# Other places for the seven-product and eight-product weight pairs of a decoder trunk, and their splits interleaved

## Chip, cores and metric

The kernel runs on one core of one Trainium2 chip. The metric is the device time of one execution in microseconds (us). The kernel before takes 2254.26 us, the median of three runs (2252.91 to 2255.19).

## What is computed

The reference is a decoder trunk of two layers for 256 tokens of width 2048, in fp32. Each layer has a token mixer (HGRN2 in the first, gated linear attention, "GLA", in the second), which shares its input projection with a cross-attention into 256 memory tokens; an output projection; and a SwiGLU feed-forward network of 5632 hidden columns. Cut to what matters:

```
x = x + concat(mixer(norm(x) @ w_in), memory_attention(xq, mem)) @ w_out
g, u = split(norm(x) @ w_gate_up)        # 5632 columns each
x = x + (silu(g) * u) @ w_down
# GLA: q, k (768 columns each), v, g (1536 each), gk_low (16), xq (512) = norm(x) @ w_in
```

In the GLA layer the last 16 + 512 columns of the input projection are the low-rank decay and the queries of the memory attention ("gx" in the kernel); gk0 and gk1 are its key and query columns for two heads each.

## The kernel before

**Products.** Every number is held as a high and a low part (fp32r), and every product of two tiles is three matmuls: high by high, high by low, low by high. A weight is loaded raw into a buffer `raw` of four blocks of 512 columns (three such buffers), and `split` (L276) makes its parts: ScalarE (ACT) casts the high part, VectorE (DVE) subtracts to get the low one. Parts of two blocks lie in one of six buffers, a single block in one of two. The traces call the parts of pair i parts<i>a, b, c and d. TensorE (PE) multiplies and sums in eight PSUM banks.

**Pairs.** Weight rows go by pairs of two tiles of 128 rows, 2048 rows being eight pairs, and two column blocks (gate and up, say) are computed together. A pair of kind "S" goes by a scheme of Strassen and Winograd with seven products (21 matmuls for 256 tokens). Kinds "O" and "H" (and "-" in the mixer) take eight (24 matmuls). The seven products need sums of weights. `seven` (L451) makes them: it splits a single block (a), splits two (b), subtracts in place on `raw` (one block, then two), splits two blocks (c), and splits the last two (d). An O pair needs only a and b, an H pair one subtraction of one block and a third split c besides.

**Loads.** For an S pair of the feed-forward network `load_pair` has SyncE's queue (SP) load one row of blocks (L443), GpSimd's queue (POOL) add a second row onto it as an accumulating transfer (L444), and SP load the rest (L445, L447). The accumulating transfer waits until the first row has landed, and the subtraction on VectorE until both have. An O or H pair has plain loads (L445, L449). For pair 0 of an S-headed block, and for pair 7 where it is S, that sum lies in a tile T of its own, loaded by GpSimd's queue (`load_apart`, L428 and L429).

**Gate and up.** `project_halves` (L624) does 512 gate and 512 up columns as one block; a layer has eleven blocks b. KINDS (L1197) is a table of the kinds of the eight pairs: one entry each for b = 0, 1, 2, 3, and the last one for all after. From block 1 on, `Engine.kept` holds the instructions of TensorE, VectorE and ScalarE in program order, so the order of the code is the order on the engine. The seven sums of a block are combined by VectorE (`sums`, L1223), then gated, transposed and split into the operand of the down projection (L1266), four 512-column pieces per part, two of which run behind each block. These steps fall due at keys (WHEN, L1203) that `mark` passes as the pairs go by. Two down splits per block run on GpSimd (L300) rather than VectorE; each is held back by `free_port` until a certain add of `sums` has run.

**Mixer.** In the GLA layer `gla` (L1139) computes gx by two calls of `project` (four quads of tiles, 264 columns each time, eight products for a pair), `gla_pair` (L1068) computes gk0 and gk1 by `project_two` (L549), with the plan "------S-", one pair on seven. The order of work outside blocks 1 to 10 is a scheduler's.

Of the kernel before, what the change touches and what calls it, by code (L numbers as in the profile page):

```python
# [17 lines left out]
P = 128  # L18
# [22 lines left out]
def trunk_kernel(ctx: ExitStack, tc: tile.TileContext, x, mem, norm_mix, norm_ffn, norm_mem,  # L41
# [234 lines left out]
    def split(src, name, by=2, turned=False):  # L276

        if isinstance(src, list):
            both = wts.tile([P, 2, 2, 512], F32R, tag="parts", name=f"parts{name}", bufs=6)
            for k in (1, 0):  # L280
                hi = both[:, 0, k:k + 1, :]
                ac.activation(out=hi, in_=src[k], func=AF.Copy, scale=-1.0)
                ve.scalar_tensor_tensor(out=both[:, 1, k:k + 1, :], in0=src[k], scalar=-1.0, in1=hi.bitcast(F32),
                                        op0=ALU.mult, op1=ALU.subtract)
            return [(both[:, 0, k, :], both[:, 1, k, :]) for k in range(2)]
# [165 lines left out]
    def seven(i, raw, fed, between=None):  # L451

        n = raw.shape[2]
        tt = ve.tensor_tensor
        b00, = split(raw[:, 0:1, :], f"{i}a")
        b11, b10 = split(raw[:, 2:4, :], f"{i}b")
        if between:
            between()

        if not fed:  # L460
            tt(out=raw[:, 1, :], in0=raw[:, 1, :], in1=raw[:, 2, :], op=ALU.add)
        apart = fed if fed and fed is not True else None
        tt(out=raw[:, 0, :], in0=apart[:, 0, :] if apart else raw[:, 1, :], in1=raw[:, 0, :], op=ALU.subtract)
        tt(out=raw[:, 2:4, :], in0=raw[:, 2:4, :], in1=raw[:, 0:1, :].broadcast_to([P, 2, n]), op=ALU.subtract)
        t6, t7 = split([raw[:, 0:1, :], apart] if apart else raw[:, 0:2, :], f"{i}c", turned=True)
        t5, t4 = split(raw[:, 2:4, :], f"{i}d")
        return {1: ("x00", b00), 2: ("x01", b10), 3: ("z", b11), 4: ("x11", t4), 5: ("s", t5), 6: ("u", t6), 7: ("d0", t7)}
# [81 lines left out]
    def project_two(pairs, plan, w, c0, c1, n, name, give, view=lambda ps: ps, onto=None, prep=None, behind=None,  # L549
# [43 lines left out]
        for at, (p, kind) in enumerate(zip(order, plan)):  # L593
            i, raw = new_raw()
            if i == 0:
                load_pair(raw, w, p, c0, c1, n, kind, fed)
            if prep:
                prep(at)
            if i > 0:
                load_pair(raw, w, p, c0, c1, n, kind, fed)  # L600
            if kind == "S":
                todo = held(behind, seven, i, raw[:, :, 0:n], fed) if behind else seven(i, raw[:, :, 0:n], fed)
                last = at == plan.rindex("S")
                for b in (1, 6, 7, 5, 2, 4, 3) if last else (3, 2, 1, 6, 7, 5, 4):
                    product(b, pairs[p].get(todo[b][0]), todo[b][1])
                if last and at == len(plan) - 1:
                    early()
                elif len(pending) > MANY:
                    step()
                continue  # L610
# [13 lines left out]
    def project_halves(forms, kinds, w, c0, c1, name, key, keep, apart):  # L624
# [15 lines left out]
        for p, kind in enumerate(kinds):  # L640
            Engine.kept = keep <= p
            i, raw = new_raw()
            if p == 4 and kinds[7] == "S":
                apart[7] = load_apart(w, 7, c1)
            fed = apart.get(p, True)
            load_pair(raw, w, p, c0, c1, 512, kind, fed)
            x = forms[p].get
            last = p == len(PAIRS) - 1
            if kind == "S":
                todo = seven(i, raw, fed, lambda: mark(key + p))  # L650
                for b in (1, 2, 6, 7, 5, 4, 3) if last else (1, 3, 2, 6, 7, 5, 4):
                    product(b, x(todo[b][0]), todo[b][1])
            else:
                b00, b01 = split(raw[:, 0:2, :], f"{i}a")
                mark(key + p)
                b11, b10 = split(raw[:, 2:4, :], f"{i}b")
                todo = [[(2, "x00", b00), (5, "x10", b01), (4, "x10", b00), (3, "d0", b01)]]
                if kind == "O":
                    todo.append([(2, "x01", b10), (5, "x11", b11), (4, "x11", b10), (3, "d1", b11)])
                else:  # L660
                    ve.tensor_tensor(out=raw[:, 3, :], in0=raw[:, 3, :], in1=raw[:, 2, :], op=ALU.subtract)
                    e1, = split(raw[:, 3:4, :], f"{i}c")
                    todo.append([(2, "x01", b10), (3, "x01", b11), (7, "x11", b11), (4, "x11", e1)])
# [403 lines left out]
    def gla_pair(w, pr, dec, decay, hq, r, yq):  # L1067
# [46 lines left out]
        project_two(hq["pairs"], ("------S-", "------S-")[pr], w, kw + pr * 2 * DK, pr * 2 * DK, 2 * DK, f"gk{pr}", give,  # L1114
# [24 lines left out]
    def gla(hq, scale, yq):  # L1139
# [11 lines left out]
        psx = [project(hq, range(NQ), w, 3 * MIX + i * half, half, f"gx{i}",  # L1151
                       prep=lambda q: len(got) == 0 and q == 3 and got.append(scale())) for i in range(2)]
# [3 lines left out]
        for t in range(NT):  # L1156
            ac.activation(out=low[:, t, 0:GR], in_=psx[0][t][:, 0:GR], func=AF.Copy, scale=r[:, t:t + 1])
# [30 lines left out]
        attention(1, [[(0, psx[0][t][:, GR:half]), (half - GR, psx[1][t][:, 0:half])] for t in range(NT)], r, yq)  # L1188
# [8 lines left out]
    KINDS = ("SHHSHOSO", "HHHSSOSO", "SHHSSOSO", "SSHSSOHS", "SSSSSOSS")  # L1197
# [10 lines left out]
    def ffn(l, forms, r, after, tail=None):  # L1208
# [9 lines left out]
        def up_block(b):  # L1218
            ps = project_halves(forms, KINDS[min(b, 4)], w_gate_up[l], 512 * b, DFF + 512 * b, f"f{l}_{b}_",
# [4 lines left out]
            def sums():  # L1224
# [4 lines left out]
                for out, p, q in ((s0, 2, e0), (e1, 6, e0), (s1, 7, e1), (e1, 5, e1), (e0, 5, s1),  # L1229
                                  (s1, 4, s1), (e1, 3, e1)):  # L1230
                    ve.tensor_tensor(out=out, in0=ps[p], in1=q, op=ALU.add)
                    if p in (2, 5) and out is not e0 and b:
# [201 lines left out]
```

## Time and profile before

| what | value |
|---|---|
| median of three runs | 2254.26 us |
| the profiled execution, its own time | 2254.6 us |
| span of its instructions | 2252.8 us |
| busy, PE / DVE / ACT / POOL | 99% / 90% / 64% / 12% |
| granted clock of TensorE | 0.999 |
| matmuls recorded | 10668 |
| HBM read | 472.12 MB |

A row of a timeline gives start, duration, engine, line of the kernel, operation, and tiles as out<-in; in brackets stands how long the engine was idle before, and what it was released by. Durations on PE overlap, since matmuls are pipelined; the spacing of their starts is the cost. Rows of VectorE overlap by about 0.1 us in the same way. PEld is the load of a matmul's weights.

### The profile page before, as it was taken

What the parts mean: (1) busy time and instruction counts of PE and PEld (TensorE: products, weight loads), DVE (VectorE), ACT (ScalarE), POOL (GpSimd) and SP (SyncE); (2) the same over time, 40 slices, a digit from 0 to 9 for tenths busy, and PEclk for the clock granted to TensorE, in tenths of its full rate; (3) what the DMA queues carried; (4) which work ended last, traced back from release to release, by engine and by line L of the source; (5) the groups of instructions that cost most, each with busy time, mean ns of one, the idle gap of its engine ahead of it and who ended that gap; (6) DMA issues with size and microseconds to landing.
All of it is one profiled execution on the core that took longest, in us unless ns stands there. A gap on an engine that the chain in (4) does not pass through costs nothing.

```text
span 2252.8 us, 30400 instructions
## 1 busy us (share of the span) xinstructions
PE 2238.6 (99%) x10668; PEld 1894.6 (84%) x10668; DVE 2031.5 (90%) x2551; ACT 1452.8 (64%) x2010; POOL 280.4 (12%) x275
## 2 busy tenths in 40 slices
PE   9999999999999999999999999999999999999998
PEld 7888888888888888888889999988888888888887
DVE  6879899898998999999996887889999999999997
ACT  7656656565666666666665665566566676666664
POOL 1000100000111112112210000000011221212110
PEclk9999999999999999999999999999999999999999
DMA  8656655656687778878865445566677878887874
GB/s 296 215 168 213 199 182 177 200 193 190 198 236 232 229 234 231 230 230 238 244 221 168 141 156 182 164 209 197 208 221 224 233 230 238 242 238 236 231 233 167
DMA packets 255628, 477.28 MB, mean 212 GB/s; under 512 B 18255, under 2 KB 47731, under 8 KB 255219
## 3 DMA queue, kind: packets, MB, share of 16 engines
q1 hardware_dynamic: 228547, 420.21, 55.5%
q0 software_dynamic: 25632, 50.87, 13.0%
q10 hardware_dynamic: 1296, 4.26, 0.5%
q8 instruction: 84, 1.38, 0.2%
q14 instruction: 69, 0.57, 0.1%
HBM read 472.12 MB, written 3.15 MB: 211 GB/s over the span
## 4 chain that ended last, share of the span: by engine, by line
PE 90%; DVE 6%; issue 2%; DMA 1%; ACT 1%; SPq 0%; POOL 0%; DVEq 0%; POOLq 0%; ACTq 0%
PE f_p L151 34%; PE fd L151 18%; PE wo L151 4%; PE m1p L151 2%; PE hv2p L151 2%; PE hv1p L151 2%; PE hf0p L151 2%; PE hv0p L151 2%; PE wo1p L151 2%; PE hf2p L151 2%; PE hf1p L151 2%; PE wo0p L151 2%; PE m0p L151 2%; PE gk0p L151 1%; PE gk1p L151 1%
## 5 line engine op out<-in xcount | busy, mean ns | idle before, releaser
L151 DVE TENSOR_TENSOR raw<-raw 128x1024 f32<-128x1024 f32 (+3 forms) x330 | 311.2, 943 | 16.7 <-DMA raw<-in_w_down_dram 5.6
L151 ACT CAST parts<-raw 128x1024 fp32r<-128x1024 f32 (+1 forms) x216 | 211.7, 1016 | 56.8 <-DMA raw<-in_w_down_dram 14.7
L151 DVE TENSOR_TENSOR parts<-raw,parts 128x1024 fp32r<-128x1024 f32 (+1 forms) x176 | 200.2, 1171 | 22.7 <-ACT parts L151 22.0
L444 POOL DMA_DIRECT2D raw<-in_w_gate_up_dram x92 | 80.4, 873 | 541.2 <-DMA raw<-in_w_gate_up_dram 274.7
L300 POOL TENSOR_TENSOR parts<-raw,parts 128x1024 fp32r<-128x1024 f32 x40 | 95.6, 2406 | 113.5 <-ACT parts L151 81.2
L151 ACT COPY h<-fd 128x512 f32<-128x512 f32 x80 | 45.7, 588 | 46.5 <-PE fd L151 44.0
L428 POOL DMA_DIRECT2D T<-in_w_gate_up_dram x36 | 21.1, 587 | 430.2 <-DVE hf_4g L151 82.7
L151 ACT ACTIVATE s<-s,rf_r 128x512 f32<-128x512 f32 x44 | 31.8, 723 | 42.0 <-DVE s L151 42.0
L151 DVE SCALAR_TENSOR_TENSOR s<-e,rf_r,s 128x512 f32<-128x512 f32 x44 | 45.7, 1076 | 2.9 <-ACT s L151 0.5
L151 DVE TENSOR_TENSOR e<-f_p,e 128x512 f32<-128x512 f32 x66 | 45.2, 684 | 2.6 <-DVE s L151 0.5
L429 POOL DMA_DIRECT2D T<-in_w_gate_up_dram x36 | 31.0, 861 | 120.4 <-DMA T<-in_w_gate_up_dram 111.1
L151 ACT COPY fd<-h 128x512 f32<-128x512 f32 x82 | 45.2, 582 | 0.0
L444 POOL DMA_DIRECT2D raw<-in_hgrn_w_in_dram x17 | 14.7, 867 | 209.9 <-DMA raw<-in_hgrn_w_in_dram 124.6
L151 PE MATMUL fd<-parts,s_0h 128*128 128x512 f32 x128 | 39.8, 392 | 0.0
L151 PE MATMUL fd<-parts,s_4h 128*128 128x512 f32 x128 | 39.8, 392 | 0.0
L151 PE MATMUL fd<-parts,s_8h 128*128 128x512 f32 x128 | 39.8, 392 | 0.0
L151 PE MATMUL fd<-parts,s_2h 128*128 128x512 f32 x128 | 39.8, 392 | 0.0
L151 PE MATMUL fd<-parts,s_6h 128*128 128x512 f32 x128 | 39.8, 392 | 0.0
L151 PE MATMUL fd<-parts,s_1h 128*128 128x512 f32 x128 | 39.4, 389 | 0.0
L151 PE MATMUL fd<-parts,s_3h 128*128 128x512 f32 x128 | 39.4, 389 | 0.0
L151 PE MATMUL fd<-parts,s_5h 128*128 128x512 f32 x128 | 39.4, 389 | 0.0
L151 PE MATMUL fd<-parts,s_7h 128*128 128x512 f32 x128 | 39.4, 389 | 0.0
(6020 smaller groups left out, 7434.0 us busy)
## 6 DMA issues: line engine op xcount, KB each, us to landing
raw<-in_w_gate_up_dram SPq DMA_DIRECT2D x224, 512.0 KB, 4.4
raw<-in_w_down_dram SPq DMA_DIRECT2D x80, 1024.0 KB, 5.5
raw<-in_w_gate_up_dram SPq DMA_DIRECT2D x220, 256.0 KB, 4.2
raw<-in_hgrn_w_in_dram SPq DMA_DIRECT2D x79, 512.0 KB, 4.6
raw<-in_gla_w_in_dram SPq DMA_DIRECT2D x96, 384.0 KB, 3.3
raw<-in_w_gate_up_dram POOLq DMA_DIRECT2D x92, 256.0 KB, 4.9
T<-in_w_gate_up_dram POOLq DMA_DIRECT2D x72, 256.0 KB, 5.0
raw<-in_w_out_dram SPq DMA_DIRECT2D x16, 1024.0 KB, 5.1
```

The source lines that it names most:

```text
L151: ins = func(*args, **kwargs)
L300: low = (nc.gpsimd if free_port else ve).tensor_tensor(out=both[:, 1, k:j, 0:m], in0=src[:, k:j, :], in1=both[:, 0, k:j, 0:m].bitcast(F32) ...
L428: nc.gpsimd.dma_start(out=both[:, 0, :], in_=rows[0])
L429: nc.gpsimd.dma_start(out=both[:, 0, :], in_=rows[1], accum_op=ALU.add)
L444: nc.gpsimd.dma_start(out=raw[:, 1, 0:n], in_=rows[1], accum_op=ALU.add)
```

## The change

1. *The next S pair's start is interleaved.* `seven` gets a function `ahead`, called between its splits c and d (and in an H pair ahead of split c): it takes a buffer, issues the next pair's loads, and makes its split a. A pair that was begun so does its first subtraction ahead of split b. Where the sum lies apart in T, the subtraction on two blocks is put between the two halves of split c.
2. *Order of pairs.* From block 1 on the pairs go 0, 1, 2, 5, 3, 4, 6, 7; the O pair (5) comes fourth instead of sixth.
3. *KINDS.* Blocks 1 and 2 have one S pair more each, in the place of an H pair. Block 3 takes the plan of the blocks after it, two S more. That is four pairs in each of two layers.
4. *GLA projections.* gk0 and gk1 go by "-----SS-", two pairs on seven. gx becomes one call of `project_two` with the same plan for both of its 264-column halves, and the sums end in two tiles of SBUF (tags gate and v) instead of in PSUM.
5. *Sums.* The seven adds run in another order, and GpSimd's two splits are released by the first and the fourth add (e1 + bank 6, e0 + bank 5) instead of the first (s0 + bank 2) and the fourth (e1 + bank 5).

```diff
-    def seven(i, raw, fed, between=None):
+    def seven(i, raw, fed, between=None, b00=None, ahead=None):
...
+        if not begun:
+            b00, = split(raw[:, 0:1, :], f"{i}a")
...
+        if fed and begun:
+            less()
         b11, b10 = split(raw[:, 2:4, :], f"{i}b")
...
+        if not (fed and begun):
+            less()
+        if apart:
+            t6, t7 = split([raw[:, 0:1, :], apart], f"{i}c", turned=True, between=both_less)
+        else:
+            both_less()
+            t6, t7 = split(raw[:, 0:2, :], f"{i}c", turned=True)
+        if ahead:
+            ahead()
         t5, t4 = split(raw[:, 2:4, :], f"{i}d")
...
-        for p, kind in enumerate(kinds):
-            Engine.kept = keep <= p
-            i, raw = new_raw()
...
+        def ahead(at):
+            if at < len(order) and kinds[order[at]] == "S":
+                i, raw = come(at)
+                came.append((i, raw, split(raw[:, 0:1, :], f"{i}a")))
+
+        for at, p in enumerate(order):
+            kind = kinds[p]
+            Engine.kept = keep <= at
+            i, raw, begun = came.pop() if came else (*come(at), None)
...
-        project_two(hq["pairs"], ("------S-", "------S-")[pr], w, kw + pr * 2 * DK, pr * 2 * DK, 2 * DK, f"gk{pr}", give,
+        project_two(hq["pairs"], "-----SS-", w, kw + pr * 2 * DK, pr * 2 * DK, 2 * DK, f"gk{pr}", give,
...
-        psx = [project(hq, range(NQ), w, 3 * MIX + i * half, half, f"gx{i}",
-                       prep=lambda q: len(got) == 0 and q == 3 and got.append(scale())) for i in range(2)]
+        psx = []
...
+        project_two(hq["pairs"], "-----SS-", w, 3 * MIX, 3 * MIX + half, half, "gx", give,
+                    prep=lambda at: at == 4 and got.append(scale()), fed=False)
...
-    KINDS = ("SHHSHOSO", "HHHSSOSO", "SHHSSOSO", "SSHSSOHS", "SSSSSOSS")
+    KINDS = ("SHHSHOSO", "HHSSSOSO", "SSHSSOSO", "SSSSSOSS", "SSSSSOSS")
+
+    ORDERS = ((0, 1, 2, 3, 4, 5, 6, 7), (0, 1, 2, 5, 3, 4, 6, 7))
...
-                for out, p, q in ((s0, 2, e0), (e1, 6, e0), (s1, 7, e1), (e1, 5, e1), (e0, 5, s1),
+                for out, p, q in ((e1, 6, e0), (s0, 2, e0), (s1, 7, e1), (e0, 5, s1), (e1, 5, e1),
                                   (s1, 4, s1), (e1, 3, e1)):
                     ve.tensor_tensor(out=out, in0=ps[p], in1=q, op=ALU.add)
-                    if p in (2, 5) and out is not e0 and b:
+                    if (p == 6 or out is e0) and b:
                         free_port.append(ve.last)
```

On VectorE, in a steady block (5 of the first layer), before: the fourth and fifth pairs, 139 and 140, are S, and the sixth, 141, is O; SCALAR_TENSOR_TENSOR is the split c, raw<-raw are the subtractions.

```order
L151 TENSOR_TENSOR parts139d<-raw_6691,parts139d 128x1024
L151 TENSOR_TENSOR parts140a<-raw_6731,parts140a 128x512
L151 TENSOR_TENSOR parts140b<-raw_6731,parts140b 128x1024
L151 TENSOR_TENSOR raw_6731<-raw_6731 128x512
L151 TENSOR_TENSOR raw_6731<-raw_6731 128x1024
L151 SCALAR_TENSOR_TENSOR parts140c<-raw_6731,parts140c 128x1024
L151 TENSOR_TENSOR parts140d<-raw_6731,parts140d 128x1024
L151 TENSOR_TENSOR parts141a<-raw_6774,parts141a 128x1024
L151 TENSOR_TENSOR parts141b<-raw_6774,parts141b 128x1024
```

The same engine and block after: 139 is now the O pair, 140 and 141 are S.

```order
L151 TENSOR_TENSOR parts138d<-raw_6639,parts138d 128x1024
L151 TENSOR_TENSOR parts139a<-raw_6703,parts139a 128x1024
L151 TENSOR_TENSOR parts139b<-raw_6703,parts139b 128x1024
L151 TENSOR_TENSOR parts140a<-raw_6736,parts140a 128x512
L151 TENSOR_TENSOR parts140b<-raw_6736,parts140b 128x1024
L151 TENSOR_TENSOR raw_6736<-raw_6736 128x512
L151 TENSOR_TENSOR raw_6736<-raw_6736 128x1024
L151 SCALAR_TENSOR_TENSOR parts140c<-raw_6736,parts140c 128x1024
L151 TENSOR_TENSOR parts141a<-raw_6755,parts141a 128x512
L151 TENSOR_TENSOR parts140d<-raw_6736,parts140d 128x1024
L151 TENSOR_TENSOR raw_6755<-raw_6755 128x512
L151 TENSOR_TENSOR parts141b<-raw_6755,parts141b 128x1024
```

The O pair has moved up by two places, split a of pair 141 stands ahead of split d of pair 140, and the first subtraction of 141, which needs both of its accumulated rows, ahead of its split b.

On TensorE, at the start of gx, before: fd is the last down projection of the first layer, tp_hm are the transposes of the mixer's input.

```order
L151 MATMUL fd_5_3_0_1_9861<-parts_2_9919,s_10l 128x512
L151 MATMUL gx_0_0_9957<-parts_0_9961,hm_0x 128x264 x3
L151 MATMUL gx_0_1_9958<-parts_0_9961,hm_0x 128x264 x3
L151 MATMUL gx_0_0_9957<-parts_0_9961,hm_0x 128x264 x3
L151 MATMUL gx_0_1_9958<-parts_0_9961,hm_0x 128x264 x3
L151 MATMUL tp_hm_6_9980<-ident,h 128x128
```

The same place after:

```order
L151 MATMUL fd_5_3_0_1_9873<-parts_2_9931,s_10l 128x512
L151 MATMUL tp_hm_6_9979<-ident,h 128x128
L151 MATMUL tp_hm_7_9989<-ident,h 128x128
L151 MATMUL gxp_9998<-parts216a,hm_2x 128x264 x3
L151 MATMUL gxp_10002<-parts216a,hm_2x 128x264
```

The twelve matmuls of gx that stood between the last fd and the first transpose have moved behind it.

On VectorE, at the end of gx, after (gxgate and gxv are the two tiles of its sums; before, no such row stood there):

```order
L151 TENSOR_TENSOR parts224a<-raw_10301,parts224a 128x2x384
L151 TENSOR_TENSOR gxgate<-gxp_9998,gxgate 128x264
L151 TENSOR_TENSOR gxgate<-gxp_10002,gxgate 128x264
L151 TENSOR_TENSOR gxv<-gxp_10006,gxv 128x264
L151 TENSOR_TENSOR gxv<-gxp_10010,gxv 128x264
```

Four adds on VectorE now stand between the last product of gx and the scaling of the queries on ScalarE.

## Prediction before the run

> **What bounds the kernel now.** I read the page first (span, busy shares), then the waits of TensorE, the chain of waits in order of time, the windows of the feed-forward blocks, and last the timelines of one block and of the two places in the mixer that the change touches. Page:
>
> ```profile
> span 2252.8 us, 30400 instructions
> PE 2238.6 (99%) x10668; PEld 1894.6 (84%) x10668; DVE 2031.5 (90%) x2551; ACT 1452.8 (64%) x2010; POOL 280.4 (12%) x275
> ```
>
> TensorE (PE) is busy for 99%, VectorE (DVE) for 90%. What TensorE waited for, with total, times and longest in us:
>
> ```profile
> PE tgk L151 <- ACT gsk L151: 1.4, 2, 0.8
> PE tp_hm L151 <- DVE h L151: 1.0, 2, 0.8
> PE f_p L151 <- DVE parts96c L151: 0.3, 1, 0.3
> ```
>
> The waits are crumbs, so the time is the number of matmuls times their spacing. The chain has stretches of matmuls without a gap (start, length, count); the last three are 512, 264 and 384 columns wide:
>
> ```profile
> 791.29 38.81 PE f_p L151 x171
> 1216.45 14.66 PE gx L151 x120
> 1261.60 14.04 PE gk0p L151 x81
> ```
>
> That is 38.81/171 = 227 ns, 14.66/120 = 122 ns and 14.04/81 = 173 ns per matmul. Now blocks 1 to 5 of the first layer's gate/up work (window, length, busy time with count of PE, PEld, DVE, ACT and POOL, clock, DMA share, GB/s):
>
> ```profile
> 559.40:614.30 54.90, 54.55 (x248) 44.85 (x247) 50.63 (x59) 35.02 (x46) 7.95 (x6) 1.00 0.61 194
> 614.30:666.90 52.60, 52.60 (x238) 43.63 (x237) 47.83 (x52) 35.25 (x47) 10.35 (x9) 1.00 0.79 236
> 666.90:729.70 62.80, 62.80 (x283) 52.09 (x282) 56.66 (x63) 40.19 (x52) 11.63 (x12) 1.00 0.79 236
> 729.70:791.10 61.40, 61.40 (x276) 50.91 (x275) 58.81 (x64) 41.77 (x54) 10.67 (x10) 1.00 0.79 231
> 791.10:852.60 61.50, 61.50 (x277) 50.94 (x275) 58.76 (x64) 41.77 (x54) 11.97 (x11) 1.00 0.79 227
> ```
>
> From block 4 on, TensorE is never idle although VectorE carries 58.8 of 61.5 us. Its granted clock is 1.00, so matmuls get no cheaper.
>
> **The change part by part.** *Matmuls removed.* A product is three matmuls. A pair on seven products (S) has 21, on eight (O, H) 24. Per layer, block 1 gains one S pair, block 2 one, block 3 two: 4 x 3 x 2 layers = 24 matmuls of 512 columns. Each of the two gk projections gains one S pair: 6 of 384. The gx query projection was 192 matmuls of 264 and becomes 6 x 24 + 2 x 21 = 186: 6 of 264. Sum: 24 x 0.227 + 6 x 0.173 + 6 x 0.122 = 5.45 + 1.04 + 0.73 = **7.2 us off**. All of it lies on the path, since TensorE is the path, as long as its operands stay ahead.
>
> Against this stands a rule of the Trainium skill (TensorE: Matmul & The Clock Gate, Back-to-back issue gap): in a stream of weight loads and matmuls, one of 512 columns is spaced about 131 ns, and only an isolated one about 216 ns. By it the 24 matmuls would be worth 3.1 us. The result would then be 2.3 us later than mine, no change that can be told. The trace disagrees (227 ns over 171 in a row), the measurement decides, and I give it no chance of its own.
>
> *VectorE work added.* One S pair, one O pair and the head of the next S pair in block 5 (start, duration):
>
> ```profile
> 806.14 1.23 DVE L151 TENSOR_TENSOR parts139d<-raw,parts139d 128x1024 fp32r<-128x1024 f32 x1
> 807.29 0.68 DVE L151 TENSOR_TENSOR parts140a<-raw,parts140a 128x512 fp32r<-128x512 f32 x1
> 807.89 1.22 DVE L151 TENSOR_TENSOR parts140b<-raw,parts140b 128x1024 fp32r<-128x1024 f32 x1
> 809.02 1.95 DVE L151 TENSOR_TENSOR raw<-raw 128x512 f32<-128x512 f32 x2
> 810.98 1.23 DVE L151 SCALAR_TENSOR_TENSOR parts140c<-raw,parts140c 128x1024 fp32r<-128x1024 f32 x1
> 812.17 1.23 DVE L151 TENSOR_TENSOR parts140d<-raw,parts140d 128x1024 fp32r<-128x1024 f32 x1
> 813.31 1.22 DVE L151 TENSOR_TENSOR parts141a<-raw,parts141a 128x1024 fp32r<-128x1024 f32 x1
> 814.44 1.22 DVE L151 TENSOR_TENSOR parts141b<-raw,parts141b 128x1024 fp32r<-128x1024 f32 x1
> 815.58 0.69 DVE L151 TENSOR_TENSOR parts142a<-raw,parts142a 128x512 fp32r<-128x512 f32 x1
> 817.32 1.95 DVE L151 TENSOR_TENSOR raw<-raw 128x512 f32<-128x512 f32 x2
> ```
>
> Start to start an S pair (140) takes 813.31 - 807.29 = 6.02 us of VectorE and 21 x 0.227 = 4.77 of TensorE; an O pair (141) takes 2.27 and 5.45. So VectorE loses 1.25 us to TensorE in each S pair and regains 3.18 in an O. An H pair is an O with two further 512-column steps of 0.60 (807.89 - 807.29): 3.47. An S in place of an H adds 2.5 us to VectorE.
>
> Block 3 gets the very plan of blocks 4 on, whose rows show TensorE fully fed: nothing. Block 2 has room (47.8 of 52.6). Block 1 is the tight one: 50.6 + 2.5 in about 54. It already has a stall:
>
> ```profile
> 583.51 0.40 PE L151 MATMUL f_p<-parts96c,hf_4h 128*128 128x512 f32 x1
> 584.26 0.50 PE L151 MATMUL f_p<-parts96c,hf_4h 128*128 128x512 f32 x1 [0.35 <-DVE parts96c L151]
> ```
>
> 0.75 instead of 0.23 us: 0.5 lost. The plan after has three S pairs in a row, not two, but begins them behind an O that gives 3.18. I take the stall as unchanged, between 0.5 better and 1.0 worse in each layer.
>
> *The new order of pairs* in steady blocks (S S S O S S S S for S S S S S O S S) and the first split issued ahead. Counted from the start of a block, the lead of VectorE over TensorE falls by 5 x 1.25 = 6.3 us before the O now, and the row shows it used up: the split of 140c ends at 810.98 + 1.23 = 812.21, and at that time TensorE begins with it:
>
> ```profile
> 812.21 0.63 PE L151 MATMUL f_p<-parts140c,hf_4h 128*128 128x512 f32 x2
> ```
>
> After, it falls by 3.75, rises by 3.18 and falls by 4 x 1.25, to -5.57 at worst: some 0.7 us of lead at the narrowest place, where there was none (an estimate from these rows). The same operations are issued in either order, so this gives no time in blocks that lose none now. Loads move too, which is the first rival. The order of the sums and of the two adds that release GpSimd's splits shifts each release by one add of 0.6: nothing.
>
> *The gx projection.* At its start TensorE had 12 matmuls to cover the last add onto h:
>
> ```profile
> 1205.87 1.37 DVE L151 TENSOR_TENSOR h<-fd,h 128x512 f32<-128x512 f32 x2 [0.67 <-PE fd L151]
> 1206.35 1.60 PE L151 MATMUL gx<-parts,hm_0x 128*128 128x264 f32 x12
> 1207.79 0.27 PE L151 MATMUL tp_hm<-ident,h 128*128 128x128 f32 x1
> ```
>
> In the new program the two transposes stand right behind the last fd matmul. The first add ends near 1205.87 + 0.69 and TensorE is free at 1206.35; that leaves 0.2, and I add 0.15 for passing the signal on, a choice: +0.35, with bounds 0.2 and 1.0 (the whole 1.0 of the two waits for h above). At its end the scaling on ScalarE read the sum in PSUM at once:
>
> ```profile
> 1229.50 1.62 PE L151 MATMUL gx<-parts,hm_7x 128*128 128x264 f32 x12
> 1230.79 0.85 ACT L151 ACTIVATE xs<-gx,rm_r 128x264 f32<-128x264 f32 x2 [0.26 <-PE gx L151]
> 1230.96 0.27 PE L151 MATMUL tx<-ident,xs 128*128 128x128 f32 x1
> ```
>
> Now an add on VectorE stands between, 264 columns, by half of the 0.68 of a 512-column step some 0.35 us, with signals on both sides: +0.9, bounds 0.4 and 1.4. The further splits and subtractions of the two S pairs go beside the matmuls, since VectorE is not the busy engine there (gx, then the stretch with the first gk projection):
>
> ```profile
> 1206.30:1231.00 24.70, 24.70 (x206) 24.66 (x206) 14.46 (x24) 14.72 (x29) 0.71 (x1) 1.00 0.59 184
> 1231.00:1262.00 31.00, 31.00 (x179) 29.64 (x178) 24.34 (x44) 16.85 (x35) 0.78 (x2) 1.00 0.49 153
> ```
>
> 14.5 of 24.7 us and 24.3 of 31.0. Each gk projection, with an S pair for an O, adds by the ratio of 384 to 512 columns about 0.75 x (6.02 - 2.27) = 2.8 us of VectorE: covered by the 6.7 that are idle. Were that cover gone, it would cost what exceeds it, at most the 2.8 each. The 1.4 us of waits behind gsk stay in the sum as they are; at best they go.
>
> *Sum.* The profiled execution took 2254.6 us, 1.8 more than its span and 0.3 above the median of 2254.26. 2254.6 - 7.2 + 0.35 + 0.9 = 2248.65 against that execution, **2248.3** against the median.
>
> **Rivals.** *A: the accumulated rows come too late.* An S pair's second row is added by a GpSimd transfer that waits for the first to land; VectorE's subtraction ("less") reads it, and all splits behind wait in VectorE's queue. One such chain, free (first two rows), one beside other traffic (last two), and the landing:
>
> ```profile
> 807.40 0.34 SPq L443 DMA_DIRECT2D raw<-in_w_gate_up_dram  x1
> 810.67 0.86 POOL L444 DMA_DIRECT2D raw<-in_w_gate_up_dram  x1 [9.18 <-DVE raw L151]
> 795.35 0.33 SPq L443 DMA_DIRECT2D raw<-in_w_gate_up_dram  x1
> 800.62 0.86 POOL L444 DMA_DIRECT2D raw<-in_w_gate_up_dram  x1 [7.04 <-DVE parts138c L151]
> raw<-in_w_gate_up_dram POOLq DMA_DIRECT2D x92, 256.0 KB, 4.9
> ```
>
> 3.3 or 5.3 us to the second issue, 4.9 to land: 8.2 to 10.2. Before, the load of 807.40 has until the subtraction of pair 142 at 817.32: 9.9 us; that of 795.35 until 809.02: 13.7. After, the pair at place five of a steady block takes the buffer released by d of place two, and its subtraction comes after O, a, b, subtractions and c of place four, its own a, and d of place four: 2.27 + 0.60 + 1.13 + 1.95 + 1.19 + 0.60 + 1.14 = 8.9 us. Chain 10.2: VectorE stalls 1.3, of which 0.7 is lead, 0.6 goes to TensorE in each of 16 steady blocks: +9.6, 2257.9, still the same time as before. Chain 11.2 (half of the 2.0 between the rows once more): 1.6 x 16 = +25.6, 2273.9. It costs TensorE from 9.6 us on, and the kernel is slower from 10.3 on. For it: GpSimd also issues the separate row of pair 7 in order ahead of it, and the DMA share is 0.79. Against it: the load stands right behind an O, whose loads hold no accumulation, and there the free 8.2 was seen. The Trainium skill (Perfetto Trace Analysis, Tensor Engine Instruction) says that DVE, ACT and GPSIMD are strict FIFO, while TensorE has a limited reorder; by that rule nothing slips past the stalled subtraction. The rows of VectorE above agree: each split runs in the program's order.
>
> *B: the matmuls go, but TensorE waits for the splits instead.* Block 1's three S in a row, 1.0 us more in each layer; both gk pairs, 2.8 each uncovered; the starts and ends of gx at their upper bounds, +1.15. That gives 2248.3 + 2.0 + 5.6 + 1.15 = 2257.1: the same as before. For it: the stall in block 1. Against: the windows' idle time of VectorE in the mixer.
>
> *C: the change does not do what it says*, that is, it removes no matmul: excluded, as the plans fix the count.
>
> **How the numbers follow.** Forecast 0.60; B or A with a chain between 9.6 and 10.3 (no change) 0.24; A beyond that (slower) 0.16. A measurement of this kernel can tell 0.2%, 4.5 us: faster means below 2249.8, slower above 2258.8. Range: downward the stalls of block 1 (1.0 for both layers), the 1.4 behind gsk and lower charges at gx (0.65) give 2245.2; upward it reaches to A with a chain of 10.2, 2257.9, which takes B in and leaves out 0.16 above.
>
> **What would show it.** Right: 36 matmuls fewer, the stretches of f_p still at 227 ns in blocks 4 on without waits, blocks 3 at 61.4 instead of 62.8, waits of about 0.35 and 0.9 around gx. Wrong: waits of TensorE for the c or d splits of the fifth pair, with VectorE's subtraction there released by a transfer (A); waits for splits in block 1 or gk0p (B).

## The result and the profile after

The changed kernel takes 2302.98 us (median of five runs, 2301.33 to 2307.22), against 2254.26 us before: a ratio of 1.0215, 95% interval 1.0204 to 1.0227. It is 2.2% slower, where 2248.3 us with a range up to 2257.9 was forecast. Span and TensorE on the page after:

```profile
span 2301.2 us, 30455 instructions
PE 2254.5 (98%) x10632; PEld 1883.4 (82%) x10632; DVE 2054.5 (89%) x2595; ACT 1464.6 (64%) x2027; POOL 288.8 (13%) x283
```

The 36 matmuls are gone from the records (10668 to 10632), yet the span has grown by 48.4 us. The profile names who waits. The first row is the largest group in which VectorE waited for transfers (total us, times, longest). Of the two waits of TensorE below it, the first is mostly one wait, at the end of gx; the second is one of many alike, about 1 us at a split c of a gate/up block:

```profile
DVE raw L151 <- DMA raw<-in_w_gate_up_dram: 51.1, 28, 2.7
```

```profile
PE tx L151 <- ACT xs L151: 2.0, 2, 1.8
PE f_p L151 <- DVE parts143c L151: 1.0, 1, 1.0
```

Before, VectorE had one such wait for gate/up weights, of 0.4 us. Of the new ones twenty stand at the same place, the sixth pair, one in each block from 1 on in both layers; they make up 45 of the 51 us. The windows of blocks 2 to 5 of the first layer, columns as before:

```profile
616.30:668.20 51.90, 51.90 (x235) 42.98 (x233) 48.75 (x52) 35.28 (x45) 10.44 (x9) 1.00 0.78 233
668.20:734.70 66.50, 63.54 (x277) 50.40 (x276) 61.45 (x68) 42.57 (x56) 11.93 (x11) 1.00 0.75 225
734.70:798.40 63.70, 62.40 (x277) 50.63 (x276) 57.47 (x62) 41.77 (x54) 11.98 (x11) 1.00 0.76 225
798.40:862.50 64.10, 62.61 (x277) 50.62 (x276) 59.68 (x66) 41.73 (x54) 12.81 (x12) 1.00 0.78 232
```

Only block 2 is shorter (51.9 for 52.6). Block 3 lasts 66.5 instead of 62.8, and blocks 4 and 5 about 64 instead of 61.5. TensorE now has idle time in blocks 3 to 5. In blocks 4 and 5, whose plan has no S pair more, VectorE is busy for at most 1 us longer than before.

The time went as follows, by the first matmul of each block in the two traces, both layers together: blocks 4 to 10 +33.9 us, block 3 +6.5, blocks 0 and 1 +2.6, block 2 -0.9, the GLA mixer up to the second feed-forward network +2.9, the ends of the down projections and the tail +2.5, the start of the kernel +0.9. The sum is 48.4.

In block 5 after, VectorE at the sixth of eight pairs, 141 (start, duration, idle before and what ended it):

```profile
808.61 1.22 DVE L151 TENSOR_TENSOR parts139a<-raw,parts139a 128x1024 fp32r<-128x1024 f32 x1
816.32 1.22 DVE L151 TENSOR_TENSOR parts140d<-raw,parts140d 128x1024 fp32r<-128x1024 f32 x1
...
820.11 0.69 DVE L151 TENSOR_TENSOR raw<-raw 128x512 f32<-128x512 f32 x1 [2.58 <-DMA raw<-in_w_gate_up_dram]
```

The first loads of that pair and of the next on SyncE's queue, and the accumulating transfers of both on GpSimd's:

```profile
808.72 0.34 SPq L445 DMA_DIRECT2D raw<-in_w_gate_up_dram  x1
...
810.99 0.33 SPq L445 DMA_DIRECT2D raw<-in_w_gate_up_dram  x1
```

```profile
813.37 0.86 POOL L446 DMA_DIRECT2D raw<-in_w_gate_up_dram  x1 [5.89 <-DMA raw<-in_w_gate_up_dram]
817.62 0.86 POOL L446 DMA_DIRECT2D raw<-in_w_gate_up_dram  x1 [3.39 <-DMA raw<-in_w_gate_up_dram]
```

Issue at 808.72, accumulation issued 4.65 us later, subtraction released at 820.11: a chain of 11.4 us, in two legs of 4.65 and 6.7. VectorE was ready at 817.5, 8.8 after the issue. It stood for 2.58 us with the splits of all later pairs behind it, and TensorE paid most of it at the last pair:

```profile
834.65 0.39 PE L151 MATMUL f_p<-parts143c,hf_7h 128*128 128x512 f32 x1
836.08 0.50 PE L151 MATMUL f_p<-parts143c,hf_7h 128*128 128x512 f32 x1 [1.04 <-DVE parts143c L151]
```

The wait is seen at pair 143, but its cause lies two pairs and some 16 us earlier: TensorE works off what lead there is first.

### The profile page after: what moved, and what is told of

Its sections match the earlier page's. It is cut to its first block, busy times and chain, and to the rows that moved or that the text cites. A ratio compares the mean times of both kernels' runs of the same rounds, so it can differ in the third digit from the quotient of the medians.

```text
span 2301.2 us, 30455 instructions
## 1 busy us (share of the span) xinstructions
PE 2254.5 (98%) x10632; PEld 1883.4 (82%) x10632; DVE 2054.5 (89%) x2595; ACT 1464.6 (64%) x2027; POOL 288.8 (13%) x283
## 3 DMA queue, kind: packets, MB, share of 16 engines
q8 instruction: 83, 1.36, 0.2%
## 4 chain that ended last, share of the span: by engine, by line
PE 44%; DVE 21%; DMA 10%; issue 10%; ACT 4%; SPq 0%; ACTq 0%; POOL 0%; DVEq 0%; POOLq 0%
PE fd L151 15%; DMA raw<-in_w_gate_up_dram 9%; DVE raw L151 5%; PE f_p L151 5%; PE wo L151 4%; PE hv2p L151 2%; PE wo1p L151 2%; PE hf2p L151 2%; PE wo0p L151 2%; PE hv1p L151 1%; PE gg11p L151 1%; PE gg10p L151 1%; PE gk1p L151 1%; PE gg01p L151 1%; PE gg00p L151 1%
## 5 line engine op out<-in xcount | busy, mean ns | idle before, releaser
L151 DVE TENSOR_TENSOR raw<-raw 128x1024 f32<-128x1024 f32 (+3 forms) x350 | 328.4, 939 | 69.7 <-DMA raw<-in_w_gate_up_dram 51.1
L151 ACT CAST parts<-raw 128x1024 fp32r<-128x1024 f32 x200 | 201.5, 1047 | 41.6 <-DMA raw<-in_w_down_dram 9.3
L151 DVE TENSOR_TENSOR parts<-raw,parts 128x1024 fp32r<-128x1024 f32 x160 | 188.2, 1217 | 7.4 <-ACT parts L151 7.2
L446 POOL DMA_DIRECT2D raw<-in_w_gate_up_dram x100 | 86.5, 865 | 541.8 <-DMA raw<-in_w_gate_up_dram 239.4
L151 DVE SCALAR_TENSOR_TENSOR s<-e,rf_r,s 128x512 f32<-128x512 f32 x44 | 54.0, 1266 | 2.9 <-ACT s L151 0.5
```

The source lines that it names most:

```text
L151: ins = func(*args, **kwargs)
L446: nc.gpsimd.dma_start(out=raw[:, 1, 0:n], in_=rows[1], accum_op=ALU.add)
```

## Experiments

Theory A: the accumulated row of the pair two places behind the O comes too late. Theory B: the interleave itself stalls VectorE. Theory C: VectorE has too much to do with the added S pairs. A free chain is taken as 7.3 us: for the load of 807.40 of before, 3.3 to the second issue and 4.0 to its landing in the trace (the prediction used the 4.9 of the page). Times are medians against the kernel before on the same chip (2255.1 to 2256.4). "Steady" is the mean length of blocks 4 to 9 of the first layer, "block 3" that of block 3 there, and "mixer" the time from the first gx matmul to the second layer's first gate/up matmul, all from each run's trace.

| kernel | us | ratio, 95% | steady | block 3 | mixer |
|---|---|---|---|---|---|
| before | 2254.26 | | 61.5 | 62.8 | 353.7 |
| changed | 2302.98 | 1.0204-1.0227 | 64.0 | 66.5 | 356.6 |
| 1 old order | 2260.23 | 1.0009-1.0028 | 61.5 | 62.7 | 353.9 |
| 2 no interleave | 2273.67 | 1.006-1.009 | 62.0 | 65.0 | 354.0 |
| 3 both undone | 2268.96 | 1.004-1.007 | 61.7 | 65.1 | 355.7 |
| 4 row left out | 2260.57 | 1.001-1.0029 | 61.7 | 63.0 | 353.7 |
| 5 row summed by VectorE | 2266.27 | 1.0027-1.0061 | 62.0 | 63.7 | 354.3 |
| 6 mixer edits alone | 2259.29 | 1.0005-1.0023 | 61.5 | 62.8 | 356.3 |
| 7 as 1, no interleave in mixer | 2259.60 | 1.0007-1.0026 | 61.4 | 62.8 | 354.2 |
| 8 blocks 1, 2 and gk | 2258.91 | 1.0008-1.0027 | 61.5 | 63.2 | 354.6 |
| 9 as 1, gx as before | 2258.05 | 1.0003-1.0023 | 61.6 | 62.7 | 352.9 |
| 10 next row left out | 2304.39 | 1.0206-1.0237 | 63.8 | 65.4 | 354.7 |
| 11 less VectorE work | 2267.89 | 1.0048-1.0082 | 61.7 | 64.2 | 354.5 |
| 12 next loads late, one row | 2325.98 | 1.0301-1.0336 | 65.3 | 66.4 | 357.6 |
| 13 next loads late, all rows | 2344.16 | 1.0375-1.041 | 66.3 | 68.7 | 355.7 |
| 14 O fifth | 2296.84 | 1.0165-1.0198 | 63.6 | 66.5 | 356.2 |
| 15 blocks 1 and 2 alone | 2256.16 | 0.9994-1.0012 | 61.5 | 62.8 | 353.5 |

**1. Old order.**

```diff
-    ORDERS = ((0, 1, 2, 3, 4, 5, 6, 7), (0, 1, 2, 5, 3, 4, 6, 7))
+    ORDERS = ((0, 1, 2, 3, 4, 5, 6, 7), (0, 1, 2, 3, 4, 5, 6, 7))
```

> Old order of the pairs (O sixth) in every block; the interleave, KINDS, sums, gx and gk stay as changed. Theory A (the accumulated row of the pair two places behind the O comes about 2.5 us too late, because the O gives its buffer up early and the next pair's rows are loaded beside it): the pair behind the O has 9.2 us and a free chain of 7.3, so f_p stretches go back from 41.3 to 38.8 us, total 2252 us (2254.3 - 5.5 for the matmuls of the blocks + 2.9 that the mixer is longer in the trace). Theory B (the interleave is what stalls, because the first subtraction now stands ahead of split b): stays at 2290 to 2303. Theory C (more S pairs are too much for VectorE): stays near 2300 in blocks 1 to 3 only, 2260.

Measured 2260.2. The steady blocks are back at 61.5. So with the interleave in place 42.8 of the 48.7 us hang on the order, and theory B, by which the interleave stalls by itself, falls: TensorE loses next to nothing there. VectorE still waits for a row of the second pair in some blocks (up to 1.8 us, 7.5 in all), which its lead covers. The total stays 8 us above what was expected of A, which leaves other losses (below).

**2. No interleave, new order.**

```diff
-            if at < len(order) and kinds[order[at]] == "S":
+            if False:
```

> The interleave is taken out of the gate/up blocks (no pair begins ahead; the mixer keeps it); the new order, O fourth, stays. Theory A: the late row has 10.0 us instead of 8.9 against a chain of 11.3, so a wait of about 1.3 us on VectorE stays and 0.6 to 1.3 of it goes to TensorE in each of 16 blocks: 2262 to 2273. Theory B: all comes back, 2252. Theory C: 2260.

Measured 2273.7, at A's upper end. The same subtraction, now behind the split b of its own pair:

```profile
813.19 1.22 DVE L151 TENSOR_TENSOR parts141b<-raw,parts141b 128x1024 fp32r<-128x1024 f32 x1
814.89 1.95 DVE L151 TENSOR_TENSOR raw<-raw 128x512 f32<-128x512 f32 x2 [0.48 <-DMA raw<-in_w_gate_up_dram]
```

The wait has shrunk from 2.58 to 0.48 us: the row has one split more of time (10.0 instead of 8.8 us), and its chain is shorter too (10.5 instead of 11.4). Steady blocks are still 0.5 long, block 3 still 2.2.

**3. Both undone.** Both edits above.

> Old order and no interleave in the gate/up blocks; KINDS, sums, gx and gk stay as changed. Theories A and B: 2252. Theory C: blocks 1 to 3 keep stalls of 1 to 5 us each, 2260.

Measured 2269.0, 17 us above what A and B expect, and above experiment 1, which keeps the interleave. So in the old order the interleave gains 8.7 us; in the new order it loses 29 (2303.0 against 2273.7). C's expectation of a loss in block 3 is met: that block lasts 65.1, with TensorE waiting for c splits at three S pairs (114, 115, 116). No transfer is named there. One of these waits, VectorE's row and TensorE's:

```profile
685.46 1.22 DVE L151 SCALAR_TENSOR_TENSOR parts115c<-raw,parts115c 128x1024 fp32r<-128x1024 f32 x1
```

```profile
685.48 0.49 PE L151 MATMUL f_p<-parts115c,hf_3h 128*128 128x512 f32 x1
686.74 0.50 PE L151 MATMUL f_p<-parts115c,hf_3h 128*128 128x512 f32 x1 [0.77 <-DVE parts115c L151]
```

Block 3 and block 5 of this run have the same plan. Their first matmuls start at 668.55 and 795.38, and split c of their second pair here:

```profile
673.36 1.22 DVE L151 SCALAR_TENSOR_TENSOR parts113c<-raw,parts113c 128x1024 fp32r<-128x1024 f32 x1
```

```profile
797.21 1.23 DVE L151 SCALAR_TENSOR_TENSOR parts137c<-raw,parts137c 128x1024 fp32r<-128x1024 f32 x1 [0.49 <-ACT parts137c L151]
```

That is 4.8 and 1.8 us behind the block's start: VectorE comes to block 3 with 3.0 us less of lead. Ahead of block 3 run 48 matmuls of a down projection, 11.8 us, and ahead of later blocks 96, 22.7 us.

**4. The late row left out.** No accumulation for the sixth pair:

```diff
-                nc.gpsimd.dma_start(out=raw[:, 1, 0:n], in_=rows[1], accum_op=ALU.add)
+                if not alone:
+                    nc.gpsimd.dma_start(out=raw[:, 1, 0:n], in_=rows[1], accum_op=ALU.add)
...
+            load_pair(raw, w, p, c0, c1, 512, kinds[p], apart.get(p, True), at == 5 and order[5] == 4)
```

> As changed, but the accumulating transfer of the pair at the sixth of eight places (pair 4) is left out in the gate/up blocks from 1 on, so that this pair's sum of weights lacks its second row: its subtraction waits for the first row alone (landing about 4.6 us after issue). Theory A: the waits of 2.6 us there go, f_p stretches fall to 39 to 39.5 us, total 2252 to 2262 (the next pair's row, 10.3 to 13.5 us after its issue, may be next in line). Theories B and C: stays within 10 us of 2303.

Measured 2260.6: with everything else as changed, one transfer fewer per block takes 42.4 us away. Theory A is borne out.

**5. The same row without an accumulating transfer.**

```diff
+        def feed(at):
+            return apart.get(order[at], not (at == 5 and order[at] == 4))
...
-            load_pair(raw, w, p, c0, c1, 512, kinds[p], apart.get(p, True))
+            load_pair(raw, w, p, c0, c1, 512, kinds[p], feed(at))
...
-                todo = seven(i, raw, apart.get(p, True), lambda: mark(key + at), begun and begun[0], lambda: ahead(at + 1))
+                todo = seven(i, raw, feed(at), lambda: mark(key + at), begun and begun[0], lambda: ahead(at + 1))
```

> As changed, but the pair at the sixth of eight places (pair 4, in blocks from 1 on) has both of its rows loaded plainly by SyncE's queue and summed by VectorE (0.6 us more of VectorE in each block), in place of the accumulating transfer. Theory A (that row's late landing is the loss): a plain load lands 4 to 6 us after its issue, well inside 8.9, so f_p stretches of steady blocks fall from 41.3 to 38.8 to 39.4 and the total to 2258 to 2266, like the kernel with the row left out (2260.6) or a little later. If VectorE's load were the loss (theory C), 0.6 us more of it would make it later than 2303.

Measured 2266.3, a hair beyond A's range. More work for VectorE makes the kernel 36.7 us faster: it was not its load but its wait. The steady block is 0.3 longer than in experiment 4, so about half of the added 0.6 us shows.

**10. The next pair's accumulation left out instead.**

```diff
-            load_pair(raw, w, p, c0, c1, 512, kinds[p], apart.get(p, True), at == 5 and order[5] == 4)
+            load_pair(raw, w, p, c0, c1, 512, kinds[p], apart.get(p, True), at == 6 and order[5] == 4)
```

> As changed, but the accumulating transfer of the seventh pair in order (pair 6) is left out in the gate/up blocks from 1 on, instead of that of the sixth, so pair 6 lacks its second row. If the sixth pair's row lands late because two accumulating transfers overlap, its chain falls from 11.3 to 7.5 to 9 us, the wait on VectorE from 2.6 to under 0.5, and the total to 2255 to 2262. If its own plain loads and those of the seventh pair (which start 2.3 us behind) make it late, the chain stays above 10.5 and the total above 2285.

Measured 2304.4: no change against 2303.0, and chains of 10.5 us and more in the steady blocks. The seventh pair's accumulating transfer is not what draws the chain out. That of the fifth pair, ahead of it, was left in.

**12 and 13. The next pair's plain rows held back**, in 12 the first of them alone, in 13 all (`late` is set for the seventh pair in blocks 3 to 10).

```diff
+        def hold(ins):
+            if late:
+                tc.add_manual_dep(ins.ins, subtracted[0], mybir.DependencyInfo(
+                    mybir.DependencyClass.Sync, mybir.DependencyReason.DATA), reason="late")
...
-        nc.sync.dma_start(out=raw[:, 0:4:3, 0:n], in_=w[2 * p * P:(2 * p + 2) * P, c0:c0 + n].rearrange("(k p) c -> p k c", p=P))
+        hold(nc.sync.dma_start(out=raw[:, 0:4:3, 0:n], in_=w[2 * p * P:(2 * p + 2) * P, c0:c0 + n].rearrange("(k p) c -> p k c", p=P)))
...
```

> As changed, but in blocks 3 to 10 the loads of the seventh pair in order wait until VectorE has made the first subtraction of the sixth, so that they no longer run beside the sixth pair's accumulating transfer. Nothing is left out. If those plain loads, 2.3 us behind the sixth pair's own, are what draws its chain out from 7.3 to 11.3 us, the chain falls to 7.3 to 8, the wait at the sixth pair goes, and the same chain of the seventh pair becomes late instead (it starts about 6.5 us later than in the changed kernel): a wait of about 2 us there, total 2290 to 2305. If something else draws it out, the chain stays above 10.5, both pairs wait, and the total is above 2320.

> As the kernel before this one, but all four plain rows of the seventh pair wait for the first subtraction of the sixth (there only the first row of them did, and the other three still ran beside the sixth pair's transfer; its chain was 9.5 to 11.2 us). If those rows draw the chain out, it is 7.2 to 8 us here, VectorE does not wait at the sixth pair (8.9 are allowed), and waits about 2 to 3 us at the seventh instead. If it stays at 10 or more, the cause is in the sixth pair's own path.

Run 12 was inconclusive: the pair's other rows went ahead of the held one. The total of 2325.98 and the waits at both pairs are as its second expectation has them; the chain, 9.7 to 11.3 us in the steady blocks, fits neither. Run 13 holds all of them. In its block 5 the sixth pair's chain on SyncE's queue, GpSimd's and VectorE:

```profile
814.93 0.34 SPq L452 DMA_DIRECT2D raw<-in_w_gate_up_dram  x1
```

```profile
819.46 0.86 POOL L453 DMA_DIRECT2D raw<-in_w_gate_up_dram  x1 [5.88 <-DMA raw<-in_w_gate_up_dram]
```

```profile
823.77 0.69 DVE L151 TENSOR_TENSOR raw<-raw 128x512 f32<-128x512 f32 x1
...
833.73 0.69 DVE L151 TENSOR_TENSOR raw<-raw 128x512 f32<-128x512 f32 x1 [1.95 <-DMA raw<-in_w_gate_up_dram]
```

The subtraction at 823.77 waits for nothing: the row was there within 8.84 us, and the accumulation took at most 4.3 us instead of 6.7. So about 2.5 of the 4 us by which the chain exceeds a free one came from the next pair's plain rows. The other blocks agree: over blocks 4 to 10 of both layers the second leg took 5.9 to 7.0 us in the changed kernel and 4.1 to 4.2 here (4.8 in one), as it did before at the pair behind the O (3.9 to 4.2). The first leg is still 4.5 to 5.1 instead of 3.3, so the chain is not the 7.2 to 8 that was expected, and VectorE still waits 0.1 to 0.5 us in most of these blocks (1.0 in one). The wait has moved to the seventh pair, as expected. The whole is slower, which says nothing against it: the held rows came late for everyone behind.

**14. O fifth.**

```diff
-    ORDERS = ((0, 1, 2, 3, 4, 5, 6, 7), (0, 1, 2, 5, 3, 4, 6, 7))
+    ORDERS = ((0, 1, 2, 3, 4, 5, 6, 7), (0, 1, 2, 3, 5, 4, 6, 7))
```

> As changed, but the O pair goes fifth (order 0, 1, 2, 3, 5, 4, 6, 7 from block 1 on). Theory A says that the pair two places behind the O is the one that is late, if it has an accumulated row: with O fifth that is the seventh (pair 6), with the same 8.9 us, so VectorE waits 2 to 2.7 us there and the total is 2285 to 2305. With O sixth (as before) it is pair 7, whose sum lies apart, and nothing is late. If being fourth were what matters (the place in the block, not what stands two behind), O fifth lies near the old order, 2260 to 2270.

Measured 2296.8, inside A's range. The wait has moved by one pair, to the seventh:

```profile
823.19 0.69 DVE L151 TENSOR_TENSOR raw<-raw 128x512 f32<-128x512 f32 x1 [1.24 <-DMA raw<-in_w_gate_up_dram]
```

This run also shows what goes with a long first leg. The sixth pair's load stands right behind the O's here, and its first leg is 3.2 to 3.4 us in the steady blocks; the seventh's stands behind an S pair's, which holds an accumulation, and takes 4.4 to 5.6. No run changed that neighbour alone, so the cause of this part is not shown.

In the order before, two places behind the O stood pair 7, whose sum is loaded into a tile of its own well ahead. The old place of the O was the one at which this chain does not exist.

**6, 7, 9. The mixer.** In 6 the gx and gk edits are made to the kernel before. In 7 the interleave is taken out of `project_two` in the kernel of experiment 1; in 9 gx there is as before.

```diff
-                more = (lambda: ahead(at + 1)) if plan[at + 1:at + 2] == "S" else None
+                more = None
```

> The kernel before with the gx and gk edits alone (two pairs on seven in each, no interleave anywhere). By the prediction's own terms: 1.8 us of matmuls off, 1.25 on at gx: 2253.7. By the trace of the changed kernel, where TensorE waits about 2 us at the end of gx and the matmuls behind run at 322 instead of 173 ns for 3 us: 1.8 off, 2 to 4 on: 2254.5 to 2256.5.

> Old order of pairs as in the first experiment (2260.2), and no interleave in project_two (mixer, output projection, last down projection); the gate/up blocks keep it. If the interleave there costs time (the stretch fd_0p is 21.5 and 22.1 us in that run, 20.5 and 20.4 before), it goes back: 2256 to 2258. If not: 2260, and the wait behind fd_0p has another cause.

> Old order of the pairs as in the first experiment (2260.2), and gx by two passes of project again, as before the change; gk stays at two pairs on seven. In the first experiment TensorE waits 1.84 us at the end of gx and 0.27 at its start; both go, and 6 matmuls of 264 columns (0.7) come back: 1.4 less, 2258.5 to 2259.5. If the edit of gx is worth what the prediction says (0.7 off, 1.25 on), 0.5 less.

Measured 2259.3, 2259.6 and 2258.1. The first is later than expected: the mixer lasts 2.6 us longer than before, not 0.5 less. Some 1.7 of that stands in two later projections (gg00p and gg10p), which the edits leave alone; why is open. The second shows no gain to be told (2260.2 without it): the longer stretch of fd_0p, in the last down projection, is not the interleave's doing, and its cause stays open. The third is some 0.5 under its range, which begins at 2258.5; its time cannot be told from that of experiment 1, so the reading rests on the traces. Its mixer lasts 352.9: 0.8 less than before, near the 1.04 that gk's six matmuls are worth. Against experiment 1 it is 1.5 less, counted from the last matmul ahead of the mixer, since the old and the new gx begin at different places. So in these traces gk pays and gx costs.

**8 and 15. What was left to keep.** Run 8 is the gate/up interleave with the old order, KINDS of blocks 1 and 2, and gk; run 15 changes one line of the kernel before:

```diff
-    KINDS = ("SHHSHOSO", "HHHSSOSO", "SHHSSOSO", "SSHSSOHS", "SSSSSOSS")
+    KINDS = ("SHHSHOSO", "HHSSSOSO", "SSHSSOSO", "SSHSSOHS", "SSSSSOSS")
```

> What the theories would keep: old order, interleave in the gate/up blocks alone, KINDS of blocks 1 and 2 as changed, block 3, sums and gx as before, gk as changed. Matmuls: 4 pairs x 3 x 0.227 = 2.7 off, gk 1.0 off, 0.5 to 1.0 for the stall of block 1: 2250 if VectorE stays ahead, 2254 if the small waits come back elsewhere.

> The kernel before with the KINDS of blocks 1 and 2 alone as changed (one S pair more in each; no interleave, old order, block 3, sums and mixer as before). The matmuls are worth 4 x 3 x 0.227 = 2.7 us. If VectorE keeps its lead in these two blocks, 2252 to 2253 and the blocks last 96.9 and 51.9 us instead of 97.6 and 52.6; if the third S pair in a row costs TensorE what it saves, 2255 to 2257 and the blocks last as before.

Run 8 gave 2258.9, above both expectations, and run 15 2256.2 (ratio 1.0003, 0.9994 to 1.0012): no gain. TensorE in block 1 of run 15:

```profile
579.27 0.50 PE L151 MATMUL f_p<-parts95c,hf_3h 128*128 128x512 f32 x1 [0.16 <-ACT parts95c L151]
580.58 0.50 PE L151 MATMUL f_p<-parts95c,hf_3h 128*128 128x512 f32 x1 [0.80 <-DVE parts95c L151]
```

The gate/up stretch of blocks 0 and 1 grows from 85.8 to 86.8 us with three matmuls fewer; block 2 gives 0.4 (40.8 to 40.4). No version was found that beats the kernel before.

**11. Less work for VectorE ahead of block 3**, on the kernel of experiment 3:

```diff
-                for t in range(NT):
+                for t in range(NT) if b != 2 else ():
                     ve.scalar_tensor_tensor(out=s[:, t, :], in0=e[:, 1 - t, :], scalar=r[:, t:t + 1], in1=s[:, t, :],
```

> Old order and no interleave in the gate/up blocks, as in the third experiment (2269.0), and the two gating multiplications of block 2 are left out in both layers (VectorE does 2.4 to 4 us less just ahead of block 3; that block's hidden columns stay ungated). If block 3 is late because VectorE comes to it with too little lead (12 us of down projection ahead of it, 23 ahead of later blocks), its f_p stretches fall from 42.4 and 41.3 to 38.8 to 40, and the total by 3 to 5 us to 2264 to 2266. If transfers make it late, they stay.

Measured 2267.9, 1.1 less instead of 3 to 5; block 3's gate/up stretches went from 42.4 and 41.3 to 41.6 and 41.3. Little of the freed time became lead: split c of the second pair starts 4.0 us behind the block's start in both layers, where it was 4.8 in the first and 4.0 in the second. The first layer's stretch lost as much as it gained in lead, and the second's neither gained nor lost, which fits lead as the cause. VectorE and ScalarE ahead of block 3:

```profile
663.28 0.69 DVE L151 SCALAR_TENSOR_TENSOR parts112c<-T,parts112c 128x512 fp32r<-128x512 f32 x1 [1.52 <-ACT parts112c L151]
```

```profile
661.45 1.27 ACT L151 COPY h<-fd 128x512 f32<-128x512 f32 x2 [1.55 <-PE fd L151]
662.61 0.64 ACT L151 ACTIVATE parts112c<-T 128x512 fp32r<-128x512 f32 x1
```

ScalarE's cast for split c stands in its queue behind a copy of the down projection's sum, which waits for TensorE. However early VectorE is, it gets this cast only then. From these rows it seems that lead can be built only between that copy and the block's first matmul: half a down projection, 5.9 us here and 11.3 in later blocks. No run tested that.

## Why the prediction was wrong

**The forecast's failed step** is the dismissal of rival A. It gave as reason against it that "the load stands right behind an O, whose loads hold no accumulation, and there the free 8.2 was seen". In the new order that is not so for the pair that is late. Ahead of its load in SyncE's queue stand those of pair 140, an S pair, whose accumulating transfer is issued 2.1 us before it:

```profile
803.30 0.34 SPq L445 DMA_DIRECT2D raw<-in_w_gate_up_dram  x1
```

```profile
806.61 0.86 POOL L446 DMA_DIRECT2D raw<-in_w_gate_up_dram  x1 [6.72 <-DVE raw L151]
```

Nor is it alone behind. The free row of before, issued at 807.40, has no other S pair's loads within 6 us behind it. In the new place the O frees its buffer after 2.27 us, and the next S pair's four rows (810.99) start beside the late pair's transfer. Run 13 shows that these rows are what stretches the accumulation. The mechanism, the place and the 8.9 us that the row is allowed were right (8.8 in the trace); the chain was taken as 8.2, at most 10.2, where it is 10.7 to 11.8 in the steady blocks, and the part of A that makes the kernel slower got 16% instead of most of the chance. The sum held nothing for it, and it cost 33.9 us in blocks 4 to 10 alone.

**A's price** was too low as well: 1.6 us per block for a chain of 11.2, after 0.7 of lead. Blocks 4 to 10 lose 2.4 each, and VectorE's waits at the sixth pair there are 1.9 to 2.7, 2.3 on average: nothing was absorbed. The estimate of 0.7 us of lead at the narrowest place is not borne out.

**"Block 3 gets the very plan of blocks 4 on ... nothing"** failed. It was forecast at 61.4, and lasts 66.5 in the changed kernel. Without the late row it still lasts 63.0 (experiment 4) or 62.7 (experiment 1): two S pairs save 1.36 us of matmuls and TensorE waits about as long. The plan is the same, the lead with which VectorE comes to it is not; that this is the cause is argued from the rows of experiments 3 and 11.

**Block 1** was named the tight one, with up to 1.0 us of loss in each layer. In the changed kernel blocks 0 and 1 lost 1.1 and 1.6 us against a forecast of 0.7 less. But this is the late row again: VectorE waits 1.8 and 2.4 us for it there, and in experiment 4, without it, the two blocks last 1.2 and 1.1 us less than before. So in the new order and interleaved, the third S pair in a row costs nothing that shows. Without both it does: run 15 shows 1.0 and 1.2 net, 0.7 saved and 1.7 and 1.9 more of waits, which is over the bound.

**The gx projection**: the start was charged 0.35 and took 0.27 (by the starts of the last fd matmul and the first transpose). The end was charged 0.9, with a bound of 1.4, and took 2.0: the first transpose starts 2.1 us behind the last gx matmul, against 0.13 before. What was missed is that ScalarE has two small scalings of the decay's columns and the queries one by one in its queue behind the adds. After, VectorE's last adds, ScalarE and TensorE:

```profile
1253.73 0.76 DVE L151 TENSOR_TENSOR gxv<-gxp,gxv 128x264 f32<-128x264 f32 x2
```

```profile
1254.87 0.50 ACT L151 ACTIVATE gk<-gxgate,rm_r 128x16 f32<-128x16 f32 x2
1255.27 0.49 ACT L151 ACTIVATE xs<-gxgate,rm_r 128x248 f32<-128x248 f32 x1
```

```profile
1255.81 0.73 PE L151 MATMUL tx<-ident,xs 128*128 128x128 f32 x2 [1.81 <-ACT xs L151]
```

TensorE's transpose starts 2.1 us after these last two adds began. The edit saves 0.73 us of matmuls and costs 2.2, a net loss of 1.5, which is what experiment 9 gives back.

**Right** were the count and price of the matmuls (the stretches without waits still run at 227 ns), gk's 1.04 us with its splits covered, and that the order by itself gains nothing in blocks that lost nothing (61.7 in the steady blocks of experiment 4, which has the new order). The sums' new order shows no cost in the steady blocks of experiment 1; by itself it wasn't run. The Trainium skill's rule, cited from Perfetto Trace Analysis, Tensor Engine Instruction, that ACT, DVE and GPSIMD are strict FIFO, is what these traces show at two places: VectorE's splits behind the subtraction (2.58 us in block 5), and ScalarE's cast behind the copy of fd, for which ScalarE waited 1.55 us.

Open is the stretch of fd_0p in the last down projection of either layer: 20.4 to 20.5 us before, up to 24.2 in other runs, 21.5 and 21.0 in the changed kernel. The start of the kernel varied by 1.4 us in runs whose code there is the same, so its +0.9 tells nothing.

## What to carry to other kernels

When steps of unequal length share a ring of buffers, a short step hands its buffer back early: look up what is loaded next beside it, and take the price of a transfer chain from a row with the same company, not from a quiet one. Moving a subtraction that needs a transfer ahead of work that needs none pays only where the transfer is early: the same interleave gained 8.7 us in the old order and lost 29 in the new, where the row was late. A plan that runs without waits in one block proves nothing for another block with less cover ahead of it.

## What the runs showed of the hardware

In the changed kernel's trace TensorE's granted clock fell to half after the 2.0 us gap at the end of gx (gaps here by the starts of matmuls; TensorE was idle for 1.81 of it). Windows of 2 to 2.5 us there:

```profile
1253.70:1256.00 2.30, 0.49 (x4) 0.23 (x2) 2.30 (x5) 1.87 (x5) 0.00 (x0) 1.00 0.70 257
1256.00:1258.00 2.00, 1.92 (x13) 1.75 (x13) 0.78 (x2) 1.69 (x4) 0.00 (x0) 0.87 0.73 182
1258.00:1260.50 2.50, 2.50 (x9) 2.50 (x9) 1.60 (x3) 0.00 (x0) 0.00 (x0) 0.50 0.49 183
```

```profile
1257.53 3.23 PE L151 MATMUL gk0p<-parts224a,hm_2x 128*128 128x384 f32 x9
```

Nine matmuls of 384 columns were spaced about 337 ns (1257.53 to 1260.56) instead of 173, some 1.5 us in all, after the gap itself was over. The same happened in runs 12, 13 and 14. The nine other runs with the new gx had gaps of the same length there (1.8 to 2.1 us) and kept a clock of 1.00, and in experiment 1, one of these, the first 24 matmuls of gk0p and the transposes between them took 4.95 us instead of 6.5. So it is no fixed price of such a gap: 4 of 13 runs paid it.
